# A hybrid decoder layer on one core: constants, working buffers and split weights moved to 64-byte and 128-byte addresses

## Chip, cores and metric

The kernel runs on one NeuronCore of a Trainium2 chip. The metric is the time of one execution on the device in microseconds, the median of several runs. The core has a matrix engine (TensorE, PE in the rows, with its weight loads as PEld), a vector engine (VectorE, DVE), a scalar engine (ScalarE, ACT), a general-purpose engine (GpSimd, POOL) and a queue engine that issues DMAs (SyncE, SP). On-chip memory, SBUF, has 128 partitions; an address below is a byte offset within a partition, the same in all 128.

## The reference

One decoder layer over 512 tokens of width 2048, in float32:

- `h = rms_norm(x)`, then one projection `h @ w_in` to 8480 columns, which are split into q, k, v and a gate for attention (1024 each), the token-shifted columns of an RWKV-7 mixer (three blocks of 1024 and 288 low-rank columns) and its gate (1024).
- Attention with 16 heads of 64: rotary q and k, causal, the union of three dilation patterns mixed by their softmax denominators.
- RWKV-7: data-dependent decay, a delta-rule state of 64 x 64 per head over the 512 tokens, a group norm and a bonus term.
- Both results are multiplied by `silu` of their gate, concatenated, projected by `w_out` (2048 x 2048) and added to `x`; a final RMS norm follows.

## The kernel before

All large products keep about float32 accuracy with a fast 4-byte matmul type: each operand is split into a high part (`hi`, a copy rounded by ScalarE) and a low part (`lo`, the difference, by VectorE), and each product is three matmuls, hi x hi, hi x lo and lo x hi. The split activations `hh0..15` and `hl0..15` (later `mh`, `ml`, in the same places, pool `hp`) are 128 x 512 each and stay in SBUF. Weights come as chunks of 1024 columns: a DMA into one of two `raw` buffers, ScalarE writes `whi`, VectorE `wlo` (three buffers each, pool `wp`; the fourth chunk and the last four go to the k4 buffers instead).

TensorE's program is a list of items. Items of kind "a" (58 tiles of 128 output columns, `mm_...`: low-rank columns, k, r, v, q/k of attention, gates) have the weight chunk as stationary operand and `hh`/`hl` as moving operand of 512 columns, 48 matmuls a tile. Items "v" (`mv`, 352 columns) and "o" (`mo`, 512 columns, the output projection), "h" and "t" (`mh` and `mt` as outputs, 256 columns, the last quarter of it) have `hh`/`hl` or `mh`/`ml` stationary and the weights moving. `mo` is 3 x 4 x 48 = 576 matmuls, `mv` 576, `mh` and `mt` 192 each.

Everything else (decay and rates, the 32-step substitution in GpSimd on `XT` and `Xtmp`, the state scan, attention scores, gates) is cut into generators that a planner, the class `Model` with one object per engine, drops between these matmuls while the program is written out. It keeps an estimated clock, and for each tile by name the time when it is ready and last read; it also picks VectorE or ScalarE for a copy (`evac`). So the order of every engine's instructions is fixed before the run.

Small matmuls that the prediction names: `pw` and `pa` (low-rank products, `wsh`/`wsl` stationary, `tws` moving), `pg` (`gh`/`gl` stationary, `g128h`, `g128l`, `g32s` moving), all 512 columns of the same data type.

Where things lie. Buffers are placed pool by pool (`hp`, `cp`, `wp`, `kp`, `sp`) in the order of their first use, each rounded up to 32 bytes; a tag with several buffers takes its largest tile as the pitch.

- `hp` begins on a 128-byte line, and its 32 tiles of 2048 bytes keep to it.
- `cp` begins on one too, with `pvt` (99 floats, 396 bytes, rounded to 416). All that follows is pushed to 32 bytes past a line: `csts`, `bmt`, `bonesr`, `hw0`, `nka`; `omu` and `warm` fall on a line again, `rstd` and `rtok` not, `ssq` (80 bytes) does, and then `xtf`, `L`, `wsh`, `wsl` and the two buffers for `tws`/`g128` lie 32 past.
- `wp`: `raw`, `whi` and `wlo` lie 32 bytes past a 128-byte line, and 160 past a 256-byte one.
- `kp`: the 20 buffers of tag k2 have the pitch of the largest tile, `W` with 8 x 65 floats, 2080 bytes, so they lie 32, 64, 96 and 0 bytes past a 128-byte line in turn; ten of 20 are off a 64-byte line. k4 (nine of 4096 bytes) and k1 (five of 1024) lie 32 past.
- `sp`: `XT` and `Xtmp` lie 32 past; small columns of one or eight floats have pitches of 32 bytes.

Of the kernel before, what the change touches and what calls it, by code (L numbers as in the profile page):

```python
# [11 lines left out]
F32 = mybir.dt.float32  # L12
F32R = mybir.dt.float32r
I32 = mybir.dt.int32
AF = mybir.ActivationFunctionType
ALU = mybir.AluOpType
# [4 lines left out]
P = 128  # L21
# [11 lines left out]
PV = {}  # L33
# [5 lines left out]
NPV = _o  # L39
# [97 lines left out]
def hymba_kernel(ctx: ExitStack, tc: tile.TileContext, xT, x, wa, wb, wo, pv, w2a2, g2, fg,  # L137
                 cst, rope, amask, bmask, out):
    nc = tc.nc
    ctx.enter_context(tc.manual_schedule())  # L140
    model = Model()
    V = Engine(model, nc.vector, 0.07, 0.00106, 0.18)
    S = Engine(model, nc.scalar, 0.06, 0.00095, 0.25)
# [6 lines left out]
    cp = ctx.enter_context(tc.tile_pool(name="cp", bufs=1))  # L150
    wp = ctx.enter_context(tc.tile_pool(name="wp", bufs=3))
    kp = ctx.enter_context(tc.tile_pool(name="kp", bufs=1))
# [5 lines left out]
    K1N, K2N, K4N, RAWN, AHEAD = 5, 20, 9, 2, 2  # L158

    def k2(shape, name, dt=F32):  # L160
        return kp.tile(shape, dt, tag="k2", bufs=K2N, name=name)

    def k1(shape, name, dt=F32):
        return kp.tile(shape, dt, tag="k1", bufs=K1N, name=name)
# [7 lines left out]
    def small(shape, name, bufs=12, dt=F32):  # L172
        return sp.tile(shape, dt, tag=f"s{shape[1]}", bufs=4 if shape[1] == 4 else bufs, name=name)

    pvt = cp.tile([P, NPV], F32, name="pvt")
    nc.scalar.dma_start(pvt, pv)

    def col(n, i):
        return pvt[:, PV[n] + i:PV[n] + i + 1]
# [5 lines left out]
    gmask = [csts[:, 320:448], csts[:, 448:576]]  # L185
    bmt = cp.tile([P, 2 * P], F32, name="bmt")
    ones = k2([P, P], "ones")
    V.memset(ones, 1.0)
    bonesr = cp.tile([P, P], F32R, name="bonesr")
    hw0 = cp.tile([P, 16], F32, name="hw0")  # L190
    nka = cp.tile([P, 8], F32, name="nka")
    omu = cp.tile([P, 27], F32, name="omu")
    V.tensor_scalar(omu, pvt[:, 0:27], -1.0, 1.0, ALU.mult, ALU.add)
    warm = cp.tile([P, 1], F32, name="warm")
    S.activation(warm, ones[:, 0:1], AF.Tanh)

    hth, htl, normed = [], [], []
    rstd = cp.tile([P, T], F32, name="rstd")
    rtok = cp.tile([P, 4], F32, name="rtok")
    xt_b, xq_b, Lb = [], [], []  # L200

    def prologue():
        acc = k2([P, T], "acc")
        xs = []

        def load_x(k):
            xs.append(k2([P, T], f"xk{k}"))
            Q.dma_start(xs[k], xT[k])
# [40 lines left out]
        for i in range(2):  # L249
            xq_b.append(dp.tile([NCH, P, 32], F32, name=f"xq{i}"))  # L250
            xt_b.append(cp.tile([P, NCH, C], F32, name=f"xtf{i}"))
            Lb.append(cp.tile([P, NCH, P], F32, name=f"L{i}"))
        start(later(), 23.7)

    def later():
        bones = k2([P, P], "bones")
        Q.dma_start(bones, cst[:, 576:704])
        Q.dma_start(bmt, bmask)
        yield 1.59, bones
        V.tensor_copy(bonesr, bones)  # L260
        V.tensor_scalar(hw0, pvt[:, PV["w0"]:PV["w0"] + 16], 0.5, None, ALU.mult)
        V.tensor_scalar(nka, pvt[:, PV["k_a"]:PV["k_a"] + 8], -1.0, None, ALU.mult)
        for i in range(2):
            G.memset(xt_b[i], 0.0)
            G.tensor_copy(Lb[i][H[i], :, H[i]], ident[H[i], H[i]][:, None, :].to_broadcast([64, NCH, C]))
            yield 0.5, G
# [136 lines left out]
    def start(gen, *wait, rank=1):  # L403
        sides.append([gen, wait_for(*(wait or (0.0,))), rank])
# [222 lines left out]
    def pre(p, r, k, v):  # L627
# [35 lines left out]
        a = k2([P, T], f"a{p}")  # L663
# [44 lines left out]
        V.tensor_scalar(rn2, rn2, 1e-24, None, ALU.max)  # L708
        V.reciprocal(rn2, rn2)
        start(subst(p, Mp, rn2), 0.06, Mp, rn2, rank=-1)  # L710
        S.activation(a, a, AF.Identity, bias=nka[:, p:p + 1], scale=col("k_a", p))
        V.scalar_tensor_tensor(k, a, 1.0, k, ALU.add, ALU.mult)
        rk = k2([P, T], f"rk{p}")
        V.scalar_tensor_tensor(rk, r, col("r_k", p), k, ALU.mult, ALU.mult)
# [47 lines left out]
    def subst(p, Mp, rn2):  # L762
        V.tensor_tensor(Mp, Mp, rn2[:, None, :].to_broadcast([P, 32, 32]), ALU.mult)
        XT = sp.tile([P, 8, 32], F32, tag="XT", bufs=2, name=f"XT{p}")
        tmp = sp.tile([P, 8, 32], F32, tag="Xtmp", bufs=1, name=f"Xtmp{p}")
        G.memset(XT, 0.0)
        for g in range(4):
            V.tensor_copy(XT.rearrange("p c t -> p (c t)")[32 * g:32 * g + 32, 8 * g:8 * g + 232:33],
                          rn2[32 * g:32 * g + 32, 8 * g:8 * g + 8])
        yield 0.1, XT  # L770
        while p >= 1 and p - 1 not in solved:
            yield 0.1
        for j in range(31):
            n = 31 - j
            G.tensor_tensor(tmp[:, :, j + 1:32], XT[:, :, j:j + 1].to_broadcast([P, 8, n]),
                            Mp[:, j, j + 1:32][:, None, :].to_broadcast([P, 8, n]), ALU.mult)
            G.tensor_tensor(XT[:, :, j + 1:32], XT[:, :, j + 1:32], tmp[:, :, j + 1:32], ALU.add)
            yield -1.5, G
        solved.add(p)
        xq = xq_b[p % 2]  # L780
        for g in range(4):
            Q.dma_start(xq.rearrange("c (q g s) t -> g (c q) s t", q=4, g=4)[g], XT[32 * g:32 * g + 32])
        start(merges(p), rank=0)
        start(build(p), rank=0)
        start(scan(p), rank=0)
# [385 lines left out]
            yield 1.05  # L1171

    fgt = []
    ssq = cp.tile([P, 4, 5], F32, name="ssq")
    yt = {}

    def residual(nb):
# [67 lines left out]
    def rkv_evac(p, which, mi, p_):  # L1245
        rkv[p, which] = shift_evac(p_, PV["mu"] + mi, f"{which}{p}")
        if which == "v":
            r, k, v = (rkv.pop((p, n)) for n in "rkv")
            start(pre(p, r, k, v), 0.0, v)
# [175 lines left out]
```

## Time and profile before

| | |
|---|---|
| Median of three runs | 1182.05 us (1180.76 to 1182.65) |
| The profiled execution | 1185.02 us, of which 1182.6 us are the span of the profile |
| Granted TensorE clock, mean | 0.992 of full speed |
| Instructions | 19112 |
| HBM read, written | 114.44 MB, 14.75 MB |

The span reaches from the first to the last instruction on the core; the rest of an execution lies around it. In the rows, `out<-in` are the program's tile names without their numbers, then come the shapes, and `x` is a count. L121 is the planner's call for TensorE, L88 that for the other compute engines, L133 for DMAs, so the line tells little and the tile names tell the place. Matmuls are pipelined: the duration of one overlaps that of the next, and the rate is read from their starts.

### The profile page before, as it was taken

To read this page: it belongs to the slowest core of one execution; us is meant where nothing else is said; L and a number is where in the kernel's file an instruction comes from. 1 tells how busy PE (TensorE), PEld (TensorE's weight loads), DVE (VectorE), ACT (ScalarE), POOL (GpSimd) and SP (SyncE) were. 2 spreads that over 40 slices of the span, in tenths; PEclk is the share of its full clock that TensorE was granted. 3 is DMA by queue.
4 is the path that set the end of the run, shared out by engine and by line. 5 is a ranking of instruction groups with operands and counts; after the bars stand their busy time and mean duration, and the time that the engine had idled before them with its cause. 6 is when DMAs were issued, how large, how long until landed. Compare 5 with 4: busy or idle time off the path is not lost. (4 is left out here: it accounts for less than half of the span.)

```text
span 1182.6 us, 19112 instructions
## 1 busy us (share of the span) xinstructions
PE 1149.7 (97%) x6878; PEld 941.8 (80%) x6878; DVE 742.1 (63%) x1522; ACT 560.8 (47%) x1243; POOL 334.1 (28%) x586
## 2 busy tenths in 40 slices
PE   7999999999999999999999999999899999999997
PEld 5877778788778878787799978777777778888897
DVE  5767866868786778778653546465557657243252
ACT  6455444555746655555533345435354445222243
POOL 1005883635627174653640000101010000011020
PEclk9999999999999999999999999999999999999999
DMA  7333342334242424324242354433445336444343
GB/s 260 119 95 114 115 124 73 103 100 121 66 138 72 118 95 125 105 87 111 63 120 61 112 158 132 124 110 107 119 134 148 116 116 215 123 125 130 102 125 143
DMA packets 89870, 139.62 MB, mean 118 GB/s; under 512 B 37936, under 2 KB 47664, under 8 KB 89776
## 3 DMA queue, kind: packets, MB, share of 16 engines
q1 hardware_dynamic: 89344, 137.83, 39.1%
q8 instruction: 54, 0.88, 0.3%
q10 hardware_dynamic: 432, 0.58, 0.1%
q14 instruction: 40, 0.33, 0.1%
HBM read 114.44 MB, written 14.75 MB: 109 GB/s over the span
## 5 line engine op out<-in xcount | busy, mean ns | idle before, releaser
L88 POOL TENSOR_TENSOR Xtmp<-XT,Mp 128x248 f32<-128x248 f32 (+30 forms) x248 | 132.4, 534 | 168.5 <-DVE XT L88 151.1
L88 POOL TENSOR_TENSOR XT<-XT,Xtmp 128x248 f32<-128x248 f32 (+30 forms) x248 | 139.3, 562 | 21.7 <-DVE XT L88 2.1
L121 PE MATMUL mm_qk<-hh,whi 128*128 128x512 f32 x256 | 104.8, 410 | 0.8 <-ACT gtok L88 0.8
L121 PE MATMUL mm_qk<-hl,whi 128*128 128x512 f32 x256 | 104.2, 407 | 0.0
L121 PE MATMUL mm_qk<-hh,wlo 128*128 128x512 f32 x256 | 104.1, 407 | 0.0
L121 PE MATMUL mm_z<-hh,wlo 128*128 128x512 f32 x256 | 103.2, 403 | 0.0
L121 PE MATMUL mm_z<-hl,whi 128*128 128x512 f32 x256 | 103.2, 403 | 0.0
L88 DVE TENSOR_TENSOR wlo<-raw_o,whi 128x512 fp32r<-128x512 f32 x64 | 48.0, 792 | 87.3 <-ACT whi L88 87.3
L121 PE MATMUL mm_z<-hh,whi 128*128 128x512 f32 x256 | 102.7, 401 | 0.0
L88 POOL TENSOR_TENSOR y<-y,fg 128x512 f32<-128x512 f32 (+1 forms) x16 | 19.4, 1244 | 253.5 <-DMA raw_o<-in_wo_dram 156.7
L88 ACT ACTIVATE ss<-ss,nm 128x128 f32<-128x128 f32 (+3 forms) x64 | 35.6, 556 | 105.4 <-DVE nm L88 100.8
L88 ACT ACTIVATE whi<-raw_o 128x512 fp32r<-128x512 f32 x64 | 36.9, 623 | 96.3 <-PE mo L121 73.4
L88 POOL TENSOR_TENSOR m<-m,m 128x512 f32<-128x512 f32 x16 | 22.2, 1410 | 213.4 <-DVE m L88 127.7
L121 PE MATMUL mo<-whi,mh 128*128 128x512 f32 x192 | 75.8, 395 | 0.0
L121 PE MATMUL mo<-whi,ml 128*128 128x512 f32 x192 | 75.8, 395 | 0.0
L121 PE MATMUL mo<-wlo,mh 128*128 128x512 f32 x192 | 75.8, 395 | 0.0
L88 DVE TENSOR_TENSOR wlo<-raw_v,whi 128x352 fp32r<-128x352 f32 (+1 forms) x80 | 49.5, 640 | 33.8 <-ACT whi L88 33.0
L88 DVE TENSOR_TENSOR wlo<-raw_qk,whi 128x512 fp32r<-128x512 f32 x64 | 45.0, 716 | 31.8 <-ACT whi L88 31.7
L121 PE MATMUL mv<-whi,hh 128*128 128x352 f32 x192 | 62.5, 326 | 1.1 <-DVE m L88 1.1
L121 PE MATMUL mv<-whi,hl 128*128 128x352 f32 x192 | 62.4, 325 | 0.0
L121 PE MATMUL mv<-wlo,hh 128*128 128x352 f32 x192 | 62.3, 324 | 0.0
L88 ACT ACTIVATE whi<-raw_v 128x352 fp32r<-128x352 f32 (+1 forms) x80 | 41.3, 543 | 38.8 <-PE mv L121 25.8
(304 smaller groups left out, 3033.9 us busy)
## 6 DMA issues: line engine op xcount, KB each, us to landing
raw_z<-in_wa_dram SPq DMA_DIRECT2D x32, 512.0 KB
raw_qk<-in_wa_dram SPq DMA_DIRECT2D x32, 512.0 KB
raw_o<-in_wo_dram SPq DMA_DIRECT2D x32, 512.0 KB
raw_v<-in_wb_dram SPq DMA_DIRECT2D x24, 352.0 KB
raw_r<-in_wa_dram SPq DMA_DIRECT2D x16, 512.0 KB
raw_v<-in_wa_dram SPq DMA_DIRECT2D x16, 512.0 KB
raw_k<-in_wa_dram SPq DMA_DIRECT2D x15, 512.0 KB
xk<-in_xT_dram SPq DMA_DIRECT2D x16, 256.0 KB
```

The lines of the kernel that those rows point to most:

```text
L88: return fn(o, *args, **kw)
L121: return fn(o, lhs, rhs, **kw)
```

## The change

No instruction is added or taken away. Eight declarations change:

- `k2` always takes a tile of 528 floats (2112 bytes, 33 x 64) and hands out a view of the shape asked for, so the 20 buffers lie 0 and 64 bytes past a 128-byte line in turn.
- `pvt` gets 112 columns (448 bytes), `rtok` 16 (64 bytes), `ssq` 4 x 8 (128 bytes).
- `nka` moves into columns 16 to 23 of `hw0`, which gets 32 columns (128 bytes).
- `warm` moves from `cp` to the small one-column buffers of `sp`, where it takes one of twelve turns.

With these sizes `csts`, `bmt`, `bonesr`, `hw0`, `omu`, `rstd`, `rtok` and `ssq` begin on 64-byte lines; `xtf`, `L`, `wsh`, `wsl`, `tws`/`g128`, `raw`, `whi`, `wlo`, k4, k1, `XT` and `Xtmp` on 128-byte lines (`raw`, `whi` and `wlo` on 256-byte lines as well). `hh`, `hl`, `mh` and `ml` do not move. The program takes 736 bytes more of each partition.

```diff
     def k2(shape, name, dt=F32):
-        return kp.tile(shape, dt, tag="k2", bufs=K2N, name=name)
+        t = kp.tile([P, 528], dt, tag="k2", bufs=K2N, name=name)
+        t = t[:, 0:math.prod(shape[1:])]
+        return t if len(shape) == 2 else t.rearrange("p (a b) -> p a b", b=shape[2])
...
-    pvt = cp.tile([P, NPV], F32, name="pvt")
-    nc.scalar.dma_start(pvt, pv)
+    pvt = cp.tile([P, 112], F32, name="pvt")
+    nc.scalar.dma_start(pvt[:, 0:NPV], pv)
...
-    hw0 = cp.tile([P, 16], F32, name="hw0")
-    nka = cp.tile([P, 8], F32, name="nka")
+    hw0 = cp.tile([P, 32], F32, name="hw0")
...
-    warm = cp.tile([P, 1], F32, name="warm")
+    warm = small([P, 1], "warm")
...
-    rtok = cp.tile([P, 4], F32, name="rtok")
+    rtok = cp.tile([P, 16], F32, name="rtok")[:, 0:4]
...
-        V.tensor_scalar(hw0, pvt[:, PV["w0"]:PV["w0"] + 16], 0.5, None, ALU.mult)
-        V.tensor_scalar(nka, pvt[:, PV["k_a"]:PV["k_a"] + 8], -1.0, None, ALU.mult)
+        V.tensor_scalar(hw0[:, 0:16], pvt[:, PV["w0"]:PV["w0"] + 16], 0.5, None, ALU.mult)
+        V.tensor_scalar(hw0[:, 16:24], pvt[:, PV["k_a"]:PV["k_a"] + 8], -1.0, None, ALU.mult)
...
-        S.activation(a, a, AF.Identity, bias=nka[:, p:p + 1], scale=col("k_a", p))
+        S.activation(a, a, AF.Identity, bias=hw0[:, 16 + p:17 + p], scale=col("k_a", p))
...
-    ssq = cp.tile([P, 4, 5], F32, name="ssq")
+    ssq = cp.tile([P, 4, 8], F32, name="ssq")
```

## Rows read from the trace of the kernel before

**Rows 1.** The page: the span, and busy time of each engine.

```profile
span 1182.6 us, 19112 instructions
...
PE 1149.7 (97%) x6878; PEld 941.8 (80%) x6878; DVE 742.1 (63%) x1522; ACT 560.8 (47%) x1243; POOL 334.1 (28%) x586
```

**Rows 2.** Who TensorE waited for: total us, times, longest; two longest and GpSimd's, of 18.

```profile
PE s L121 <- DVE kl L88: 6.4, 3, 3.5
PE mm_lora L121 <- ACT whi L88: 6.2, 2, 5.8
...
PE Y L121 <- POOL Xtmp L88: 0.2, 1, 0.2
```

**Rows 3.** The chain that ended last: start us, us, what.

```profile
1130.47 21.62 PE mh L121 x183
1152.09 23.05 PE mt L121 x192
```

**Rows 4.** Timeline of TensorE: start us, us of one matmul; three steady stretches.

```profile
970.13 0.40 PE L121 MATMUL mm_z<-hh,wlo 128*128 128x512 f32 x1
...
977.13 0.40 PE L121 MATMUL mm_z<-hh,wlo 128*128 128x512 f32 x1
...
1039.64 0.39 PE L121 MATMUL mo<-whi,ml 128*128 128x512 f32 x1
...
1046.64 0.39 PE L121 MATMUL mo<-whi,ml 128*128 128x512 f32 x1
...
1139.91 0.28 PE L121 MATMUL mh<-whi,ml 128*128 128x256 f32 x1
...
1144.11 0.28 PE L121 MATMUL mh<-whi,ml 128*128 128x256 f32 x1
```

**Rows 5.** TensorE's groups: out<-moving,stationary, shape, count | busy us, mean ns | idle before.

```profile
L121 PE MATMUL mm_z<-hh,wlo 128*128 128x512 f32 x256 | 103.2, 403 | 0.0
...
L121 PE MATMUL mo<-whi,mh 128*128 128x512 f32 x192 | 75.8, 395 | 0.0
...
L121 PE MATMUL pw<-tws,wsh 128*128 128x512 f32 x8 | 3.2, 394 | 0.0
...
L121 PE MATMUL pg<-g128h,gl 128*128 128x512 f32 x8 | 3.1, 390 | 0.0
```

**Rows 6.** VectorE's groups, columns as in rows 5.

```profile
L88 DVE TENSOR_TENSOR wlo<-raw_o,whi 128x512 fp32r<-128x512 f32 x64 | 48.0, 792 | 87.3 <-ACT whi L88 87.3
...
L88 DVE TENSOR_TENSOR wlo<-raw_qk,whi 128x512 fp32r<-128x512 f32 x64 | 45.0, 716 | 31.8 <-ACT whi L88 31.7
...
L88 DVE TENSOR_TENSOR q<-qa,q 64x512 fp32r<-64x512 f32 x16 | 11.0, 687 | 8.1 <-ACT q L88 7.7
L88 DVE TENSOR_TENSOR FT<-pF,csts 128x512 f32<-128x512 f32 x16 | 11.0, 686 | 4.1 <-PE pF L121 3.8
...
L88 DVE TENSOR_TENSOR kl<-ka,kd 128x512 fp32r<-128x512 f32 x16 | 10.5, 685 | 5.1 <-ACT kd L88 3.3 <-DMA ka<-m 1.7
...
L88 DVE TENSOR_TENSOR ml<-yl,mh 128x512 fp32r<-128x512 f32 x16 | 10.0, 685 | 0.0
```

**Rows 7.** ScalarE's groups, columns as in rows 5.

```profile
L88 ACT ACTIVATE whi<-raw_r 128x512 fp32r<-128x512 f32 x32 | 19.2, 622 | 1.2 <-PE mm_k L121 0.9
...
L88 ACT ACTIVATE mh<-yl 128x512 fp32r<-128x512 f32 x16 | 8.7, 618 | 0.0
```

**Rows 8.** The page, costliest groups: GpSimd's substitution.

```profile
L88 POOL TENSOR_TENSOR Xtmp<-XT,Mp 128x248 f32<-128x248 f32 (+30 forms) x248 | 132.4, 534 | 168.5 <-DVE XT L88 151.1
L88 POOL TENSOR_TENSOR XT<-XT,Xtmp 128x248 f32<-128x248 f32 (+30 forms) x248 | 139.3, 562 | 21.7 <-DVE XT L88 2.1
```

**Rows 9.** First 24 us: engines' busy us, TensorE clock, DMA share, GB/s.

```profile
0.00:12.00 12.00, 5.91 (x14) 4.12 (x15) 4.36 (x8) 6.08 (x10) 0.74 (x5) 1.00 0.75 244
12.00:24.00 12.00, 10.59 (x41) 7.18 (x40) 7.72 (x13) 7.30 (x13) 0.00 (x0) 1.00 0.92 301
```

**Rows 10.** The page: main DMA queue, packets, MB, share of 16 engines' span.

```profile
q1 hardware_dynamic: 89344, 137.83, 39.1%
```

## Prediction, made before the changed kernel ran

> **What bounds the kernel now.** The first view is the busy time by engine: of a span of 1182.6 us TensorE is busy for 1149.7 us (97%), VectorE for 63%, ScalarE for 47%, GpSimd for 28% [rows 1]. TensorE is idle for 1182.6 - 1149.7 = 32.9 us, and that is all that any other engine or queue can give back. The second view, who TensorE waited for, has 18 rows; the two longest are 6.4 us for `kl` (VectorE, attention) and 6.2 us for `whi` (the first weights), and GpSimd appears with 0.2 us [rows 2]; all 18 sum to 24.4 us, of which VectorE ends 15.6, ScalarE 8.6. The third view, the chain that ended last, is TensorE's own work until the last matmul ends at 1152.09 + 23.05 = 1175.14 us (`mh`, then `mt`) [rows 3]; behind it lie 7.5 us of output. 24.4 + 7.5 = 31.9 of the 32.9 us.
>
> So the time is set by the spacing of matmuls, not by any wait. The timeline gives it. In the input projections 30 matmuls of 512 columns start between 970.13 and 977.13 us, in the output projection 30 between 1039.64 and 1046.64: 233.3 ns each, both times [rows 4]. [...] From the code there are 58 tiles of 48 matmuls, 2784, of the first kind and 576 `mo`: 3360 x 233.3 ns = 784 us, two thirds of the span.
>
> **What the change moves.** No instruction, byte count, wait or queue entry is added, removed or reordered by the text of the diff; each keeps its shape and gets other addresses. Before, `hh`/`hl`/`mh`/`ml` lie on 128-byte lines already; `whi`, `wlo`, `raw`, `wsh`, `tws`, `csts`, `rstd`, `Lb`, `X`, `FT`, `q_`, `XT` begin 32 bytes past one; the 20 k2 buffers, 2080 bytes apart, lie in turn 32, 64, 96 and 0 bytes past one, so ten are off a 64-byte line. Afterwards all are on it. The sum is one question per engine: does 32 bytes past a line cost anything?
>
> *TensorE.* Its operands before are of three kinds. `mm`: moving `hh` on the line, stationary `whi` 32 past. `mo`: the other way round. `pw` and `pg`: both 32 past. If the moving operand's place cost something, `mo` would be wider spaced than `mm`, and if the stationary's did, `mm` than `mo`: both are 233.3 ns [rows 4]. If the two added, the third kind would be longest; it is shortest, 394 and 390 ns mean against 395 for `mo` and 403 for `mm_z` [rows 5] (means of one matmul with its modelled end, so only their order is used; groups of two to four are also easier to feed than a long stream). I take 0. What the rows leave open is the kind that the change makes: both on the line, in a long stream of this data type. The bounds therefore are wide. [...] Above, `mt` against `mh`, the same 256 columns from other buffers and in another order: 192 `mt` in 23.05 us are 120.1 ns each [rows 3], 36 `mh` from 1139.91 to 1144.11 are 116.7 [rows 4]. Placement or order is worth 3.4 ns there; on 3360 matmuls that is 11 us. Zero is nearest to the rows, for two opposite placements agree to a tenth of a nanosecond.
>
> *VectorE.* Four groups of one operation differ only in where they lie: `kl` (all three operands in k2, of both kinds) 685 ns, `ml` (result and one input on the line) 685, `q` (k4, 32 past) 687, `FT` (result and mask 32 past) 686 [rows 6]. The spread is 2 ns; on VectorE's 1522 operations [rows 1] that is 3 us of busy time at most, either way, and TensorE waits for VectorE for 15.6 of its 742 us busy: 0.1 us. The `wlo` subtractions do take longer, 716 ns for `raw_qk` and 792 for `raw_o` [rows 6], but both groups use the same buffers in turn, so their place is not what tells them apart. 0.
>
> *ScalarE.* `mh` (result on the line) 618 ns, `whi` (both 32 past) 622 [rows 7]. Were the 4 ns due to place, some 370 splits would save 1.5 us on an engine that is idle half the time; its longest hold on TensorE is the 6.2 us for the first `whi` [rows 2], which end with one split. 0. The constants' columns (`pvt` keeps its place, `hw0`, the new home of `nka`, `rtok`, `ssq`) are read as one element per partition, and `warm` takes one turn of the small buffers. 0; the same cover.
>
> *GpSimd.* The substitution, 248 pairs of operations of 534 and 562 ns mean [rows 8], reads and writes `XT` and `Xtmp`, now 32 past. No row shows them elsewhere. From the nearest, VectorE's 2 ns in 685, I bound it at 0.3% of 272 us, 0.8 us either way; TensorE waited 0.2 us for GpSimd [rows 2]. 0.
>
> *DMA.* In the first 24 us the DMA engines are busy for 75% and then 92% of the time, and TensorE only for 5.9 and 10.6 of 12 us each [rows 9]; this is the one stretch where a faster transfer would show. Over the run 89344 packets of the main queue take 39.1% of 16 engines' span [rows 10], 0.391 x 16 x 1182.6 / 89344 = 83 ns for 1543 bytes each; no view parts them by address. I take 0 and bound it by a tenth of a microsecond per transfer, some 30 transfers at the start, 3 us either way if all of it lay on the path; that is an outer bound, and inside the wait of 6.2 us for the first `whi`.
>
> [...]
>
> **Sum.** 0 on every line. The profiled execution took 1185.0 us, 1182.6 of it span, and is 3.0 above the median of 1182.05, whose three runs reach from 1180.76 to 1182.65. The forecast is for the median: 1182.
>
> **The rivals.**
> [...] 4% in full, 7% in part.
> [...]
> *Both operands on one line clash (slower).* Stationary and moving operand have never begun at the same place within 128 bytes in the projections; now they all do. If that puts the streams where `mt` is and not `mh`, 3360 matmuls gain 3.4 ns: 1182 + 11 = 1193. It decides from 0.7 ns a matmul on (2.4 us). For it: `mt`'s 120.1 ns. Against it: `pw`, with both operands 32 past, is not long [rows 5]. 7%.
> *The side engines fall into another rhythm.* `wlo` varies from 716 to 792 ns without a change of place [rows 6]; a few nanoseconds elsewhere can move which operations meet. Also the planner that writes out the order keeps its times by tile name, so with `nka` inside `hw0` it books the second write 0.12 us later and may choose another engine for a copy. Either moves some of the 24.4 us of waits [rows 2]; a fifth of them, 5 us, gives 1177 or 1187. 13% faster by over 0.2%, 9% slower.
> *The change doesn't do what it says*, if the pools round sizes otherwise than worked out: the same time, within "same".
>
> **How the numbers follow.** About 0.2%, 2.4 us, is what a measurement of this kernel can tell from no change. Faster: 4 + 7 + 13 = 24%. Slower: 7 + 9 = 16%. Same: 60%, with 1180 to 1184 as its own range. The range of 1176 to 1187 takes in the rhythm at both ends and leaves out the two TensorE rivals, 18%.
>
> **What would show it.** Right: spacings of 233.3 and 116.7 to 120 ns as now, `kl`, `ml` and `mh` within 2 ns of 685 and 618, TensorE busy for 1150 us and its waits near 24 us. Wrong on TensorE: a spacing of `mm` or `mo` that is off by 1 ns or more, and a busy time of TensorE that moves by as much as the span. Wrong on the side engines: TensorE's busy time stays, and its waits move by more than 2 us. Wrong on DMA: the first matmul starts earlier than 5.76 us.

## The result, and the profile after

The changed kernel takes 1191.97 us (median of five runs, 1187.83 to 1193.4) against 1182.05: a ratio of 1.0085, with a 95% interval of 1.0066 to 1.0104. It is slower by 0.85%, and outside the forecast range of 1176 to 1187. The profiled execution took 1191.97 us, the median itself; its span is 1189.7 us.

The page of the changed kernel, as [rows 1]:

```profile
span 1189.7 us, 19119 instructions
...
PE 1147.4 (96%) x6878; PEld 941.6 (79%) x6878; DVE 747.8 (63%) x1510; ACT 564.2 (47%) x1255; POOL 339.0 (28%) x586
```

TensorE's busy time falls by 2.3 us and its idle time grows from 32.9 to 1189.7 - 1147.4 = 42.3 us. The row shows something that moved addresses can't do: VectorE has 12 instructions fewer and ScalarE 12 more. Twelve copies, net, changed their engine. (The seven instructions more in all are operations on semaphores, not work.)

Who TensorE waited for in the changed kernel, total us, times, longest, as [rows 2]; seven of 20 rows:

```profile
PE s L121 <- DVE kl L88: 6.7, 4, 3.5
PE mm_lora L121 <- ACT whi L88: 6.5, 2, 5.7
PE Y L121 <- DVE A L88: 3.5, 2, 3.1
PE gp L121 <- ACT L L88: 3.1, 2, 2.2
PE zpb L121 <- DVE xnb L88: 2.9, 3, 2.3
PE gp L121 <- DVE L L88: 2.5, 1, 2.5
PE mm_k L121 <- DVE u_lora L88: 1.6, 1, 1.6
```

The two rows that led before are as they were. `gp` waiting for `L` (5.6 us in all) is new. The others were shorter in the kernel before:

```profile
PE zpb L121 <- DVE xnb L88: 1.8, 2, 1.2
...
PE Y L121 <- DVE A L88: 0.8, 1, 0.8
...
PE mm_k L121 <- DVE u_lora L88: 0.2, 1, 0.2
```

All waits sum to 33.8 us where they were 24.4: these 9.4 us are the added idle time.

TensorE's timeline in the changed kernel, start us and us of one, two steady stretches as in [rows 4]:

```profile
975.32 0.40 PE L121 MATMUL mm_z<-hl,whi 128*128 128x512 f32 x1
...
988.80 0.39 PE L121 MATMUL mm_z<-hh,wlo 128*128 128x512 f32 x1
...
1044.95 0.40 PE L121 MATMUL mo<-whi,ml 128*128 128x512 f32 x1
...
1053.35 0.40 PE L121 MATMUL mo<-whi,ml 128*128 128x512 f32 x1
```

The first two starts are 58 matmuls apart, 232.4 ns each (233.3 before); the other two 36 apart, 233.3, as before. VectorE's and ScalarE's groups keep their lengths too; of VectorE's:

```profile
L88 DVE TENSOR_TENSOR wlo<-raw_o,whi 128x512 fp32r<-128x512 f32 x64 | 48.0, 791 | 87.5 <-ACT whi L88 87.5
...
L88 DVE TENSOR_TENSOR wlo<-raw_qk,whi 128x512 fp32r<-128x512 f32 x64 | 44.8, 713 | 36.4 <-ACT whi L88 36.3
```

GpSimd's two operations are 2% longer, 545 and 571 ns where [rows 8] has 534 and 562, but no row of the changed kernel has TensorE waiting for GpSimd. So for TensorE, VectorE and ScalarE no instruction got dearer. What changed is which instruction stands where. Put side by side with the names' numbers taken off, the two traces show the same work, but the order differs in some 130 places on VectorE's queue, 100 on ScalarE's and 90 on TensorE's. TensorE's first is at about 46 us; VectorE's is at about 52 us, where a `wlo` split stands ahead of the `rtok` copy instead of behind it. Before, then after, start us and us:

```profile
52.85 0.17 DVE L88 COPY rtok<-ry_in 128x4 f32<-128x4 f32 x1
...
53.85 0.68 DVE L88 TENSOR_TENSOR wlo<-raw_k,whi 128x512 fp32r<-128x512 f32 x1
```

```profile
52.42 0.69 DVE L88 TENSOR_TENSOR wlo<-raw_k,whi 128x512 fp32r<-128x512 f32 x1
53.03 0.16 DVE L88 COPY rtok<-ry_in 128x4 f32<-128x4 f32 x1
```

The cause is in the planner: `Model.after` asks when the output tile was last written, by name, and `done` adds 0.12 us. With `nka` in its own tile the two writes follow each other; with both in `hw0` the second is booked 0.12 us later, VectorE's booked time is 0.12 us ahead for a moment, one choice falls the other way, and each later choice starts from there. That 0.12 us in the planner's books is enough for it, e3 shows below.

### The profile page after: what moved, and what is told of

Its sections match the earlier page's. It is cut to its first block, busy times and chain, and to the rows that moved or that the text cites. A ratio compares the mean times of both kernels' runs of the same rounds, so it can differ in the third digit from the quotient of the medians.

```text
span 1189.7 us, 19119 instructions
## 1 busy us (share of the span) xinstructions
PE 1147.4 (96%) x6878; PEld 941.6 (79%) x6878; DVE 747.8 (63%) x1510; ACT 564.2 (47%) x1255; POOL 339.0 (28%) x586
## 5 line engine op out<-in xcount | busy, mean ns | idle before, releaser
L88 POOL TENSOR_TENSOR Xtmp<-XT,Mp 128x248 f32<-128x248 f32 (+30 forms) x248 | 135.2, 545 | 156.0 <-DVE XT L88 138.7
L121 PEld LDWEIGHTS mm_qk<-hh,whi 128*128 128x128 f32 x256 | 49.2, 192 | 12.0 <-ACT gtok L88 1.1
```

Source lines behind the costliest of these rows:

```text
L88: return fn(o, *args, **kw)
L121: return fn(o, lhs, rhs, **kw)
```

## Order or addresses

Three kernels part the two. **e1** takes all the new addresses, but keeps `nka` a tile of its own on a 64-byte line, and so gets the order of before:

```diff
-    hw0 = cp.tile([P, 32], F32, name="hw0")
+    hw0 = cp.tile([P, 16], F32, name="hw0")
+    nka = cp.tile([P, 16], F32, name="nka")[:, 0:8]
...
-        V.tensor_scalar(hw0[:, 16:24], pvt[:, PV["k_a"]:PV["k_a"] + 8], -1.0, None, ALU.mult)
+        V.tensor_scalar(nka, pvt[:, PV["k_a"]:PV["k_a"] + 8], -1.0, None, ALU.mult)
```

> All new addresses, but nka stays a tile of its own (16 columns, 64 bytes), so the planner books as it did and every engine's instructions stand in the order of the kernel before. If the order of the instructions makes the 10 us (theory O): 1182 us, within 2 us of the kernel before, TensorE's waits near 24 us and VectorE x1522. If the addresses make it (theory A): 1190 to 1194 us with that same order.

**e2** is the kernel before with `nka` in columns 16 to 23 of a 24-column `hw0` (old addresses, order of the changed kernel):

> All old addresses (hw0 gets 24 columns, as many bytes as hw0 and nka had together, so nothing behind it moves), but nka lies in hw0, so the order is that of the changed kernel. Theory O: 1190 to 1194 us, TensorE's waits near 34 us, VectorE x1510. Theory A: 1182 us.

**e3** is the kernel before with one line of arithmetic in the planner and nothing else:

```diff
         V.tensor_scalar(nka, pvt[:, PV["k_a"]:PV["k_a"] + 8], -1.0, None, ALU.mult)
+        V.busy += 0.12
```

> The kernel before, tiles and addresses untouched; the planner alone is told that VectorE is busy 0.12 us longer after the write of nka. The order comes out as that of the changed kernel. If the sharing of one tile by hw0 and nka itself costs something on the chip (a wait between the two), this is faster than the order-only kernel; if it is the order alone (theory O), the two are equal, 1190 to 1194 us. Theory A: 1182 us.

Measured, as ratios to the kernel before: e1 1180.15 us, 0.9985 (0.9977 to 0.9994); e2 1193.4 us, 1.0095 (1.0077 to 1.0113); e3 1195.64 us, 1.0125 (1.0109 to 1.0141). By the traces e1 has every engine's instructions in the order of the kernel before, and e2 and e3 have that of the changed kernel. With it come its waits, at the old addresses; of e3's:

```profile
PE Y L121 <- DVE A L88: 3.5, 2, 3.2
PE gp L121 <- ACT L L88: 2.5, 2, 2.1
PE gp L121 <- DVE L L88: 2.5, 1, 2.5
PE mm_k L121 <- DVE u_lora L88: 1.6, 1, 1.6
```

The order alone makes the whole loss, and it can be had without touching a tile. e3 is 2.2 us above e2 with one and the same order, so a few microseconds come from something else; the mean clock below bears on it. The addresses alone bring 0.15%. The page of e1, with 1522 and 1243 instructions again:

```profile
span 1178.5 us, 19112 instructions
...
PE 1145.9 (97%) x6878; PEld 940.6 (80%) x6878; DVE 742.1 (63%) x1522; ACT 560.5 (48%) x1243; POOL 332.9 (28%) x586
```

**e4** is the changed kernel as it stands, with `V.busy -= 0.12` behind the second write to `hw0`.

> The whole change with all its new addresses, and behind the second write to hw0 the planner's booking of VectorE is taken back by 0.12 us, so that it writes out the order of before. If the order alone made the change slower: what the addresses alone gave, 0.9985 of the time before, about 1180 us, with TensorE's waits near 24 us and no row for gp waiting on L. If the home of nka inside hw0 (the one thing that e1 didn't have) costs something by itself: above 1184.

1180.02 us, 0.998 (0.9971 to 0.9989): the change as it was meant is a small gain, and the new home of `nka` costs nothing of its own.

## Is the order of before a lucky one?

**e6** adds 1.0 us in place of 0.12 and so gets a third order; **e7** changes the planner's limit, `CAP, SHARE, DEBT = 0.8, 1.4, 2.3` for 2.4, and gets one that forks off in the middle of the run. **e5** belongs to the addresses: only the pitch of the k2 buffers.

> The kernel before with its addresses, and 1.0 us added to the planner's booking of VectorE at the place where the change added 0.12. The planner then writes out a third order, that agrees with neither kernel (153 blocks of difference on VectorE against before, 151 against after). If before's order is a good draw among many and after's an ordinary one: 1188 to 1200 us. If after's order has one particular fault, that this order lacks: within 0.3% of before, 1178 to 1185.

> The kernel before with its addresses, and the planner's limit for side work on debt 2.3 instead of 2.4 us. Its order is that of before up to VectorE's instruction 810 and TensorE's 2736 (middle of the attention), then differs in 27 and 24 blocks. If the loss comes from what follows the first fork of the order in the prologue: as before, within 0.3%, 1178 to 1185 us. If any departure from before's order costs, some part of the 1.0% lies here too: 1186 to 1194.

> The kernel before with one thing of the change: the 20 buffers of 2 KB lie 2112 bytes apart instead of 2080; constants and split weights stay where they were; order of before. If the 1.5 to 1.8 us that the addresses alone gave come from VectorE's and ScalarE's operands in these buffers: about 1180 us, ratio near 0.9985. If they come from the split weights, the constants or the DMA landing places: 1181.6, ratio 1.000. The two differ by little more than a measurement can tell.

e6: 1181.24 us, 0.9995 (0.9979 to 1.001). e7: 1179.73 us, 0.9981 (0.9972 to 0.999). e5: 1181.55 us, 0.9994 (0.9985 to 1.0002). So neither of the other two orders loses anything. Only e6 speaks on the part where the changed kernel loses, though: e7's order leaves that of before at about 565 us, behind the new long waits, which lie between 59 and 560 us. One other order without the loss says that the changed kernel's has faults of its own; how common such orders are stays open. And k2's pitch alone brings no gain that can be told from nothing.

## Where the other order loses

The trace names the place of the longest new wait. VectorE's timeline in the changed kernel, start us, us, and in brackets its idle time before and who ended it:

```profile
193.46 0.41 DVE L88 TENSOR_TENSOR X<-gp,csts 128x256 f32<-128x256 f32 x1
195.67 1.23 DVE L88 TENSOR_TENSOR Mp<-Mp,rn 128x1024 f32<-128x1024 f32 x1 [1.79 <-DMA Mp<-md]
196.81 1.11 DVE L88 COPY XT<-rn 32x8 f32<-32x8 f32 x4
197.96 0.75 DVE L88 TENSOR_TENSOR X<-gp,csts 128x256 f32<-128x256 f32 x2
198.63 0.70 DVE L88 TENSOR_TENSOR wlo<-raw_z,whi 128x512 fp32r<-128x512 f32 x1
199.36 0.29 DVE L88 TENSOR_SCALAR A<-Y,wc 64x64 f32<-64x64 f32 x1
```

The multiply of `Mp` stands on VectorE's queue ahead of the copies of `A`, for which the state scan and TensorE wait. Its DMA lands late, VectorE stands 1.79 us, and the whole row behind it is late. In the kernel before, VectorE did not wait for it, and it ran 8.4 us behind VectorE's last copy of `A` for pair 0 (a pair is two of the mixer's 16 heads):

```profile
190.30 0.29 DVE L88 TENSOR_SCALAR A<-Y,wc 64x64 f32<-64x64 f32 x1
...
198.70 1.22 DVE L88 TENSOR_TENSOR Mp<-Mp,rn 128x1024 f32<-128x1024 f32 x1
```

TensorE's side of it, and its clock, in three windows (us, busy us, granted clock, DMA share, GB/s):

```profile
199.71 0.66 PE L121 MATMUL Y<-A,X 128*128 128x64 f32 x4 [3.15 <-DVE A L88]
```

```profile
198.30:201.70 3.40, 1.99 (x12) 0.99 0.31 113
201.70:205.10 3.40, 3.40 (x12) 0.51 0.37 118
205.10:208.50 3.40, 3.40 (x30) 1.00 0.49 77
```

After an idle stretch of 3.15 us the granted clock is 0.5 for 3.4 us. TensorE is busy all through it, at little more than half its pace: `mm_v` matmuls of 512 columns, one behind another, start 427 ns apart there (202.05 to 202.48 us) and 230 ns apart behind it (206.44 to 206.67). So some 1.7 us are lost on top of the wait (an estimate, half of the 3.4 us).

With that, the profiled spans of eight of the kernels come apart into idle time, half of TensorE's busy time inside half-clock stretches, and a rest:

| kernel | addresses | order | span | idle | lost to half clock | rest |
|---|---|---|---|---|---|---|
| before | old | before | 1182.6 | 32.9 | 6.8 | 1142.9 |
| after | new | after | 1189.7 | 42.3 | 6.8 | 1140.6 |
| e1 | new | before | 1178.5 | 32.6 | 5.0 | 1140.9 |
| e2 | old | after | 1188.5 | 38.3 | 8.5 | 1141.7 |
| e3 | old | after | 1189.7 | 39.8 | 8.1 | 1141.7 |
| e4 | new | before | 1177.2 | 32.5 | 3.4 | 1141.3 |
| e6 | old | third | 1179.7 | 30.4 | 6.8 | 1142.5 |
| e7 | old | late fork | 1177.8 | 32.5 | 3.4 | 1141.9 |

The rest stays within 1140.6 to 1142.9 (1139.9 to 1142.7 in the other ten profiles); all else is idle time and half clock. Against e1, which has its addresses, the changed kernel has 9.7 us more idle time and 1.8 us more of half clock, and 0.3 less of the rest: the 11.2 us by which its span is longer. In the last column the addresses show, by 1.2 us in the mean of the rows; more on that below.

One profile a kernel is a small sample of the half clock: the changed kernel's has 6.8 us of it, no more than that of before, and its second profile (e12) 8.3. The granted clock is on record for every run, though. In the mean it is 0.994 over 88 runs of the kernel before, 0.995 over the 22 of e1 and e4, 0.991 over the ten of the changed kernel (with e12's), 0.990 in e2 and 0.988 in e3. A clock lower by 0.003 over 1190 us is some 4 us of work not done (an estimate, with TensorE taken as busy all that time). So of the 10 us some 4 are half clock, and the larger part is idle time.

Now the test. First a wait put in: **e10** lets VectorE write one copy of `A` 11 times more, in the kernel before.

```diff
+                for _ in range(11 if p == 0 and c == 1 else 0):
+                    V.eng.tensor_scalar(A[0][H[0], c + 1, :], Y[H[0], 0, c % 4, :], wc[H[0], c:c + 1], None, ALU.mult)
                 for h in range(2):
```

> The kernel before in its own order and addresses; in the scan of pair 0, behind the second chunk, VectorE writes one 64x64 copy of A 11 times more (0.29 us each, 3.2 us) ahead of the copies of A that TensorE waits for. If one late copy in the scan costs TensorE its own length and a half-clock stretch behind it: a wait for A of 2.5 to 3.2 us at about 187 us that before does not have, and 1185 to 1187.5 us. If other matmuls fill such a hole or the time comes back later: 1182 to 1183.

1188.02 us, 1.0049 (1.0036 to 1.0061). That is 0.5 us above the range expected. Its waits have one new long row, and the clock was at half from 188.2 us on, within the wait, for 6.8 us, of which TensorE was busy for 4.5:

```profile
PE Y L121 <- ACT A L88: 3.2, 1, 3.2
```

A delay of 3.4 us on VectorE in this one place cost TensorE a wait of 3.2 us and the kernel 6.0 us. Then waits taken off the changed kernel, each by an edit that leaves the planner's books as they are. Four of these runs did not take away what they were meant to, and are told briefly. **e8** issued the multiply of `Mp` for pair 1 on GpSimd:

```diff
+        keep = V.eng
+        if p == 1:
+            V.eng = G.eng
         V.tensor_tensor(Mp, Mp, rn2[:, None, :].to_broadcast([P, 32, 32]), ALU.mult)
+        V.eng = keep
```

> The changed kernel in its own order; one VectorE instruction, the multiply of Mp for pair 1, that stands on VectorE at 195.67 us, waits 1.79 us for its DMA and then runs 1.23 us with the scan's copies of A behind it, is issued on GpSimd instead (the planner still books it on VectorE, so nothing else moves). If a few long waits that this order puts on TensorE are the cost: the wait of 3.1 us for A at 199.7 us and the half-clock stretch right behind it (3.4 us at 0.5, so 1.7 us lost) go, about 1187 to 1188 us. If the cost is spread over the whole order: 1191 to 1192, the wait turning up again as others.

1191.86 us, 1.0088 (1.0073 to 1.0103): the instruction at 195 us is pair 2's, and the wait for `A` stayed, 3.4 us. **e9** added two edits for the next waits, with a helper `forced` that books as `evac` does and issues on the engine named:

```diff
-                    evac(dst(h)[ro:ro + 32, :, 32 * i:32 * i + 32], z[r:r + 32, :, 32 * j:32 * j + 32])
+                    if name == "zy4":
+                        forced(V.eng.tensor_copy, dst(h)[ro:ro + 32, :, 32 * i:32 * i + 32], z[r:r + 32, :, 32 * j:32 * j + 32])
...
-                evac(L[h][H[1 - h], 4 * q:4 * q + 4, :], z[H[1 - h]])
+                if p == 3 and q == 0:
+                    forced(S.eng.copy, L[h][H[1 - h], 4 * q:4 * q + 4, :], z[H[1 - h]])
```

> As e8, and two more of the long waits taken off without moving anything in the planner's books: the first copy of L for pair 3 that ran on VectorE behind four transposes and reductions runs on ScalarE, which stood idle 2.33 us there, and the four copies of yt for pair 4 that ScalarE ran ahead of the copies of L for pair 5 run on VectorE. If a few long waits are the cost: another 1.5 us off the wait of 2.5 us at 373.6, 1 us off the one of 2.2 us at 506.4, and up to 1.7 us for each half-clock stretch behind them that no longer comes: 1182 to 1186. If spread: above 1189.

1193.45 us, 1.0089 (1.0073 to 1.0104). Those two did shorten theirs: `gp` of pair 3 from 2.5 to 1.3 us in two pieces, of pair 5 from 2.2 to 1.5; but in this profile a half-clock stretch at 201.1 stayed, and a wait for `xnb` at 559 us was 2.2 us, as in the changed kernel, with one behind it. **e12** is the changed kernel again, **e13** and **e14** as e8 and e9 with the right pair on GpSimd:

> The changed kernel itself, once more, on the same chip as the two runs that follow, to compare them with: 1190 to 1193 us by the runs so far.

> In e8 the instruction that was taken off VectorE was the multiply of pair 1; the one that stands ahead of the late copies of A at 195 us is that of pair 2, and the wait stayed (3.4 us). Here pair 2's is issued on GpSimd, which is idle there for 6.7 us; all else in the changed kernel's order. If a few long waits are the cost: the wait for A of 3.1 to 3.4 us falls under 0.5 and no half-clock stretch follows at 200 us; 4 to 6 us less than the changed kernel, 1186 to 1188. If the loss is spread over the order: less than 2 us.

> As e13, with the two other edits of e9, which did shorten their waits (2.5 to 1.3 us for pair 3's L, 2.1 to 1.5 for pair 5's). If long waits and the half-clock stretches behind them are the cost: 6 to 9 us less than the changed kernel, 1183 to 1186, with TensorE idle for 36 us instead of 42 and its busy time less 1.7 us per half-clock stretch again near 1141 us. If spread: as e13 or above.

e12 1191.88 us, 1.0081 (1.0064 to 1.0097). e13 1194.29 us, 1.0108 (1.0084 to 1.0133), e14 1193.25 us, 1.0103 (1.0083 to 1.0123). The multiply now stood at the head of GpSimd's queue until its DMA came, 14.3 us, ahead of the memset of `XT` that VectorE's next instruction needs and of pair 1's substitution; the wait for `A` grew to 4.3 us. It was moved to another queue, and the queue blocked the same way. What was wanted is in **e15**: the planner books the multiply where it did, but it is issued 20 places further down VectorE's own queue, ahead of its first reader. **e16** adds the two edits of e9.

```diff
-        V.tensor_tensor(Mp, Mp, rn2[:, None, :].to_broadcast([P, 32, 32]), ALU.mult)
+        scale = lambda *x: x
+        keep = V.eng
+        if p == 2:
+            V.eng = type("E", (), {"tensor_tensor": staticmethod(scale)})
+        late = V.tensor_tensor(Mp, Mp, rn2[:, None, :].to_broadcast([P, 32, 32]), ALU.mult)
+        V.eng = keep
...
         while p >= 1 and p - 1 not in solved:
             yield 0.1
+        if p == 2:
+            V.eng.tensor_tensor(*late)
```

> The changed kernel with one instruction moved 20 places down VectorE's queue: the multiply of Mp for pair 2, from ahead of the copies of A to just ahead of its first reader on GpSimd. In e13 it went to GpSimd and stood there for its DMA for 14 us ahead of XT's memset, so VectorE and A waited all the same (4.3 us). If long waits and the half-clock stretches behind them are the cost: the wait for A at 200 us falls under 0.7 us, no stretch of half clock follows it, and the time is 3 to 7 us under the changed kernel's 1192, so 1185 to 1189. If the loss is spread: 1190 or more.

> As e15, with the copies of L for pair 3 and of yt for pair 4 moved as in e9, which shortened those waits by 1.2 and 0.7 us. Long waits as the cause: 1183 to 1187. Spread: 1190 or more. In both cases the span should be TensorE's idle time, plus 1.7 us for each half-clock stretch, plus about 1141 us.

e15: 1190.79 us, 1.0073 (1.0053 to 1.0093). e16: 1186.0 us, 1.0033 (1.0021 to 1.0045). In e15 the wait for `A` at 200 us is down to 0.2 us and the clock is full there, yet the time hardly moves: 1190.79 us lies where the expectation put "spread", not in its 1185 to 1189. In its profile the clock is at half behind the waits for `L` of pairs 3 and 5, where that of the changed kernel has it full (columns as above):

```profile
198.30:201.70 3.40, 3.40 (x19) 1.00 0.32 100
370.50:373.90 3.40, 3.40 (x18) 0.50 0.07 12
503.60:507.00 3.40, 3.40 (x17) 0.51 0.00 0
```

So 8.5 us are lost to half clock, where the changed kernel's two profiles have 6.8 and 8.3, and over its six runs the mean clock is 0.991, as the changed kernel's. Taking that one wait away did not take half clock away with it. That the stretch moved to the next long waits is one reading; e2, with the changed kernel's order, has stretches at all three places in one profile. With those waits shortened as well, e16 has only two stretches, both in the attention part, where before has them too, and its page reads:

```profile
span 1182.0 us, 19120 instructions
...
PE 1145.3 (97%) x6878; PEld 938.7 (79%) x6878; DVE 747.6 (63%) x1513; ACT 563.0 (48%) x1252; POOL 339.4 (29%) x586
```

Idle 36.7, half clock 3.4, rest 1141.9. This profile lies 1.9 us under the median of the ten runs, whose mean clock is 0.994. One instruction moved down its queue and five copies put on another engine take 5.9 us off, about half of the 11.9 us between the changed kernel and e4. Against e4 4.2 us of idle time are left, among them `u_lora` (1.6 us) and what stayed of `gp` (3.3 us). So the long waits that the order brings, and the half clock that goes with them, are the cause: shown for this half by shortening three of them, and for the other half read from the idle time that e16 has left, which no run took off. Which of several long waits is followed by a stretch varies from profile to profile and stays open, and so does why the wait for `xnb` at 559 us is 0.9 us in some profiles of this order and 2.2 to 2.6 in others.

**e11** puts the two gains together, the repaired change of e4 with the limit of e7:

> The repaired change of e4 with the planner's limit for side work on debt 2.3 as in e7, so the order of e7 and the new addresses. If the gains of the two (0.2% each) come from different places: about 1178 us. If both are the same thing, fewer half-clock stretches: 1179.5 to 1180.5.

1177.83 us (1177.18 to 1178.62), 0.9964 (0.9952 to 0.9976): faster than both kernels, and near the first of the two figures. Against e4's profile its span is 2.0 us shorter, of which 1.4 us lie in the rest (1139.9) and 0.6 in idle time; why is not shown. Its page:

```profile
span 1175.2 us, 19112 instructions
...
PE 1143.3 (97%) x6878; PEld 940.7 (80%) x6878; DVE 739.2 (63%) x1515; ACT 563.1 (48%) x1250; POOL 332.0 (28%) x586
```

## Why the prediction was wrong

**The step that failed** is the first sentence under "What the change moves": "No instruction, byte count, wait or queue entry is added, removed or reordered by the text of the diff". The text of the diff holds no order; the planner writes it out, and it read the change. All that followed was a sum over addresses, which put the waits of TensorE at no change. The runs show the order in its place: e3 has it from one line of the planner's arithmetic, at the old addresses, and takes 1195.64 us, 1.0125; TensorE's idle time grows by 9.4 us in the changed kernel, 6.9 in e3 and 5.4 in e2.

**The right mechanism stood among the rivals and was mis-sized.** "The side engines fall into another rhythm" names the 0.12 us and the other engine for a copy. It was given 9% on the slow side and a fifth of the 24.4 us of waits, 5 us, a share that no row gave. The waits grew by 9.4 us. Two things were not in its price. A new order is not bounded by the waits that the old one has: `gp` for `L` had no row before and took 5.6 us. And a long wait can bring some 1.7 us of half clock with it. In the kernel before, the stretches at 703, 775 and 840 us each begin within 1.5 us of the end of a wait, the last one behind the 3.5 us for `kl` of [rows 2], so that price was to be read there (columns as in the windows above):

```profile
839.70:843.10 3.40, 3.40 (x9) 0.50 0.81 224
843.10:846.50 3.40, 3.40 (x19) 1.00 0.63 183
```

**The sum over addresses held.** e1 is it alone: 1180.15 us against a forecast of 1182 with "1180 to 1184 as its own range". VectorE, ScalarE and GpSimd at 0: 742.1, 560.5 and 332.9 us busy in e1, 742.1, 560.8 and 334.1 before. The first wait for `whi` is 6.0 us where it was 6.2, within the 3 us allowed for DMA. The sign that was named for DMA, a first matmul earlier than 5.76 us, was too sharp to decide anything: it starts at 5.46 to 6.19 us in the seven profiles with the old addresses and at 5.19 to 5.90 in the eleven with the new, ranges that overlap. So it can't be told from this whether the transfers came sooner. `kl`, `ml` and `mh` are 685, 685 and 616 ns in e1, within the 2 ns that were named.

**TensorE at 0 was nearly right.** In the stretch of `mm_z` the matmuls start 232.4 ns apart instead of 233.3. The rival that both operands on one line clash falls, for the projections got no slower and `mo` is 233.3 still. The argument that agreement of `mm` and `mo` to 0.1 ns leaves nothing to gain was too strong, by 0.9 ns in this stretch. Of short groups the trace of before shows starts 231.8 (`pw`) and 231.4 ns (`pa`) apart within the pairs, eight of each, and 229.6 within `pg`'s groups of four (23 spacings, without one of 307): a few nanoseconds closer than in the long stream. The price of 3.4 ns, taken from `mt` against `mh`, was not one of placement: 116.7 came from 36 of `mh`'s 192 matmuls, the 183 of [rows 3] have 118.1, and `mt` alone has 120.0 ns in the kernel before, 118.7 in e2 and 116.7 in e5, with its operands at the same places of a 128-byte line.

**The chances** put 60% on no change, because the addresses were taken for the question. The sum that they go with has no term for the order. Its 4% in full and 7% in part, and with them 11 of the 18% for TensorE, were given to a cost on every matmul that the new addresses would end. No run shows that term; what the runs show in its place is a spacing 0.9 ns shorter in the stretch of `mm_z`, about 0.6 over all the tiles of the projections, and 233.3 as before for `mo`. The criterion given for the side engines, TensorE's busy time stays and its waits move by more than 2 us, is what the trace shows: -2.3 and +9.4 us.

## What to carry to other kernels

Where a program's order is written by a planner, any edit that touches tile names, shapes or dependencies is also a change of schedule: compare the order of the instructions on each queue first, and cost the addresses only when it is the same (or hold it, as e1, e2 and e4 do, to part the two). Price a new long wait on TensorE at its length plus the half clock that may come with it (e10: 3.4 us of delay cost 6.0), and expect that taking one such wait away alone may show little (e15: 1.1 us for a wait of 3 us). When an instruction that waits for a late DMA stands ahead of what the critical engine needs, look for a place further down its own queue, as in e15, where the wait went; on GpSimd's queue, in e13, it blocked what was there.

## What was not expected of the hardware

The address gain has a place. In the same stretch of 58 `mm_z` matmuls, e1 and e5, start us and us of one:

```profile
964.45 0.39 PE L121 MATMUL mm_z<-hl,whi 128*128 128x512 f32 x1
...
977.92 0.39 PE L121 MATMUL mm_z<-hh,wlo 128*128 128x512 f32 x1
```

```profile
968.36 0.40 PE L121 MATMUL mm_z<-hl,whi 128*128 128x512 f32 x1
...
981.89 0.40 PE L121 MATMUL mm_z<-hh,wlo 128*128 128x512 f32 x1
```

(977.92 - 964.45) / 58 = 232.2 ns where `whi` and `wlo` begin on a 128-byte line (a 256-byte one as well), (981.89 - 968.36) / 58 = 233.3 where they begin 32 bytes past one; `hh` and `hl` lie on the line in both. Taken over the k, r, v, q/k and z tiles (`mm_k`, `mm_r`, `mm_v`, `mm_qk`, `mm_z`), the mean spacing of each kind lies between 232.3 and 232.9 ns in the 11 profiles with the new place and between 233.1 and 233.3 in the 7 with the old: about 0.6 ns, on 2784 matmuls 1.7 us, which is about what e1 gains (1.8 us, 0.7 to 2.7 by its interval). For `mo`, where the same buffers are the moving operand, it is 233.3 both ways in all but one profile (e11, 232.4). So with the new addresses the matmuls that have these buffers as stationary operand (512 bytes) come a little faster, and those that have them as moving operand (2048 bytes) do not. That it is the stationary operand's own place is likely but not shown: `raw` and the k4, k1 and constant buffers moved in the same runs, and only k2's pitch was tried by itself.
